# A streaming channel shuffle: the 8 KB tile is dropped, 4 and 28 KB share the first load buffer, and the last tile grows from 16 to 24 KB

## The chip, the cores and the metric

The kernel runs on one core of one Trainium2 chip. The metric is device time in microseconds (us) of one execution; the profile's span is about 1.8 us shorter than that time. Sizes such as "38 KB" are bytes per partition: 38 KB on 128 partitions is one transfer of 4864 KB. "Load" is HBM to SBUF, "store" is SBUF to HBM.

## The reference

```python
def reference(x, groups):                  # x: (16, 64, 64, 256) float32, groups = 8
    batch, h, w, c = x.shape
    x = x.reshape(batch, h, w, groups, c // groups)
    x = x.transpose(0, 1, 2, 4, 3)         # swap group and channel-in-group
    return x.reshape(batch, h, w, c)
```

Each pixel's 256 floats (1 KB) are permuted. 67.11 MB are read and 67.11 MB written, and nothing is computed.

## The kernel before

The input is cut into tiles. Each inner list of `_SLOTS` is one buffer's contents, and its numbers are KB per partition. A tile is loaded by SP's DMA queue, permuted by one vector-engine copy and stored by ACT's DMA queue. There are two load buffers and three store buffers, so a load waits for the copies of the slot two before it.

```python
_SLOTS = [[4, 8], [28]] + [[38]] * 12 + [[16]]
_IN_BUFS = 2
_OUT_BUFS = 3
# ... (pools, flat views, rows() cut)
for parts in _SLOTS:
    in_tile = in_pool.tile([P, biggest * c], F32, name="in_tile")
    out_tile = out_pool.tile([P, biggest * c], F32, name="out_tile")
    # ... (pieces: size, first row, columns)
    for q, start, cols in pieces:
        nc.sync.dma_start(out=in_tile[:, cols], in_=rows(x_flat, start, q))
    for q, start, cols in pieces:
        nc.vector.tensor_copy(out=out_tile[:, cols].rearrange("p (i j g) -> p i j g", j=CPG, g=G),
                              in_=in_tile[:, cols].rearrange("p (i g j) -> p i j g", g=G, j=CPG))
        nc.scalar.dma_start(out=rows(out_flat, start, q), in_=out_tile[:, cols])
```

Of the kernel before, what the change touches and what calls it, by code (L numbers as in the profile page):

```python
# [1 line left out]

# [4 lines left out]


F32 = mybir.dt.float32
P = 128  # L10

_SLOTS = [[4, 8], [28]] + [[38]] * 12 + [[16]]
_IN_BUFS = 2
_OUT_BUFS = 3


@with_exitstack
def kernel(
    ctx: ExitStack,
    tc: tile.TileContext,  # L20
    x: bass.AP,
    groups: bass.AP,
    out: bass.AP,
):
    nc = tc.nc
    b, h, w, c = x.shape
    G = int(groups)
    CPG = c // G
    assert G * CPG == c
    assert sum(map(sum, _SLOTS)) * P == b * h * w  # L30
    biggest = max(map(sum, _SLOTS))

    x_flat = x.rearrange("b h w c -> (b h w c)")
    out_flat = out.rearrange("b h w c -> (b h w c)")

    in_pool = ctx.enter_context(tc.tile_pool(name="in_pool", bufs=_IN_BUFS))
    out_pool = ctx.enter_context(tc.tile_pool(name="out_pool", bufs=_OUT_BUFS))

    def rows(flat, first, q):

        return flat[first * c : (first + P * q) * c].rearrange("(p f) -> p f", p=P)

    ctx.enter_context(tc.manual_schedule(engines=None))
    first = 0
# [3 lines that stand above are left out]
        at = 0  # L48
        pieces = []
        for q in parts:  # L50
            pieces.append((q, first, slice(at * c, (at + q) * c)))
            first += P * q
            at += q
# [3 lines that stand above are left out]
            nc.vector.tensor_copy(  # L57
                out=out_tile[:, cols].rearrange("p (i j g) -> p i j g", j=CPG, g=G),
                in_=in_tile[:, cols].rearrange("p (i g j) -> p i j g", g=G, j=CPG),
            )  # L60
            nc.scalar.dma_start(
                out=rows(out_flat, start, q), in_=out_tile[:, cols]
            )


# [1 line left out]
_INS = ['x', 'groups']  # L67
_OUTS = [((16, 64, 64, 256), 'float32')]

_NUMBERS = {'groups': 8}  # L70


# [26 lines left out]
```

## Time and profile before

| | before |
|---|---|
| median time | 316.1 us (3 runs at first: 316.08 to 316.41) |
| span of the profile | 314.4 us |
| HBM traffic over the span | 427 GB/s |
| vector engine busy | 38% |
| DMA engines, between first and last data packet | full |

The table says what to look at. Where the 16 DMA engines are the bound, the vector engine's idle time and the waits for loads cost nothing by themselves.

### The profile page before, as it was taken

How to read it: one execution, taken by the hardware profiler on the slowest of the kernel's cores; microseconds unless marked ns; L12 is line 12 of the kernel's file. 1: busy time of each engine (PE TensorE's matmuls, PEld its weight loads, DVE VectorE, ACT ScalarE, POOL GpSimd, SP SyncE). 2: the span in 40 equal slices, each digit the busy share in tenths (PEclk: the TensorE clock that was granted, in tenths of full speed). 3: DMA queues.
4: the chain of work that ended last, by engine and by line, in shares of the span. 5: the costliest groups of instructions: out<-in, count | busy, mean ns of one | idle time of the engine just before them, and what ended most of it. 6: DMA issues, size and time to landing. Idle time of an engine off the chain costs nothing.

```text
span 314.4 us, 132 instructions
## 1 busy us (share of the span) xinstructions
DVE 119.0 (38%) x16; POOL 0.2 (0%) x4
## 2 busy tenths in 40 slices
DVE  2081907309109109019028028037046055065400
POOL 0000000000000000000000000000000000000000
DMA  7999999999999999999999999999999999999997
GB/s 317 405 441 416 435 416 483 401 465 406 450 421 446 426 436 436 401 470 396 475 396 475 396 470 401 470 401 470 401 450 421 446 426 436 436 417 450 429 421 321
DMA packets 4608, 134.22 MB, mean 427 GB/s; under 512 B 512, under 2 KB 512, under 8 KB 768
## 3 DMA queue, kind: packets, MB, share of 16 engines
q1 hardware_dynamic: 2304, 67.11, 49.8%
q10 hardware_dynamic: 2304, 67.11, 49.4%
HBM read 67.11 MB, written 67.11 MB: 427 GB/s over the span
## 4 chain that ended last, share of the span: by engine, by line
DMA 76%; DVE 19%; issue 0%; SPq 0%; DVEq 0%
DMA in_tile<-in_x_dram 76%; DVE out_tile L57 19%; SPq L55 0%; DVEq L57 0%
## 5 line engine op out<-in xcount | busy, mean ns | idle before, releaser
L57 DVE COPY out_tile<-in_tile 128x9728 f32<-128x9728 f32 (+4 forms) x16 | 119.0, 7440 | 179.4 <-DMA in_tile<-in_x_dram 179.4
L80 POOL MEMSET const-uint8-127<- 128x1 uint8 x1 | 0.1, 103 | 0.0
L80 POOL MEMSET const-bfloat16-1.0<- 128x1 bf16 x1 | 0.1, 102 | 0.0
L80 POOL MEMSET const-float32-1.0<- 128x1 f32 x1 | 0.1, 100 | 0.0
L80 POOL MEMSET const-float32-0.0<- 128x1 f32 x1 | 0.1, 99 | 0.2 <-issue 0.2
## 6 DMA issues: line engine op xcount, KB each, us to landing
in_tile<-in_x_dram SPq DMA_DIRECT2D x12, 4864.0 KB, 37.0
out_dram<-out_tile ACTq DMA_DIRECT2D x12, 4864.0 KB, 42.6
in_tile<-in_x_dram SPq DMA_DIRECT2D x1, 3584.0 KB, 14.7
out_dram<-out_tile ACTq DMA_DIRECT2D x1, 3584.0 KB, 30.9
in_tile<-in_x_dram SPq DMA_DIRECT2D x1, 2048.0 KB, 30.4
out_dram<-out_tile ACTq DMA_DIRECT2D x1, 2048.0 KB, 15.2
in_tile<-in_x_dram SPq DMA_DIRECT2D x1, 1024.0 KB, 5.4
out_dram<-out_tile ACTq DMA_DIRECT2D x1, 1024.0 KB, 25.0
```

What stands on the lines that cost most here:

```text
L57: nc.vector.tensor_copy(out=out_tile[:, cols].rearrange("p (i j g) -> p i j g", j=CPG, g=G), in_=in_tile[:, cols].rearrange("p (i g j) -> ...
L80: nc = _bacc.Bacc("TRN2", target_bir_lowering=False, num_devices=1)
```

## The change

Its intent is one transfer pair less and more loads issued at once at the start, with the bytes of the 8 KB tile moved into the last tile.

```diff
-_SLOTS = [[4, 8], [28]] + [[38]] * 12 + [[16]]
+_SLOTS = [[4, 28]] + [[38]] * 12 + [[24]]
```

## The prediction

> **What bounds the kernel now.** I read the page first (parts 1 to 3), then the stretches of the execution, then the groups by form, then the end of the chain. Parts 2 and 3 say what kind of kernel this is:
>
> ```profile
> DVE  2081907309109109019028028037046055065400
> DMA  7999999999999999999999999999999999999997
> DMA packets 4608, 134.22 MB, mean 427 GB/s; under 512 B 512, under 2 KB 512, under 8 KB 768
> q1 hardware_dynamic: 2304, 67.11, 49.8%
> q10 hardware_dynamic: 2304, 67.11, 49.4%
> ```
>
> The vector engine works 38% of the span. The 16 DMA engines are busy in every slice but the first and the last, half for loads (q1) and half for stores (q10), 99.2% together. So the question is only whether any idle DMA time is left to win or to lose. The view by stretches cuts the span at the first and the last data packet (1.75 and 313.28 us in the trace's packet records; columns: stretch, length, vector busy, pool busy, clock, DMA share, GB/s):
>
> ```profile
> 0.00:1.75 1.75, 0.00 (x0) 0.20 (x4) 1.00 0.05 5
> 1.75:40.00 38.25, 18.50 (x4) 0.00 (x0) 1.00 1.02 425
> 40.00:280.00 240.00, 89.74 (x11) 0.00 (x0) 1.00 1.00 434
> 280.00:313.28 33.28, 10.80 (x2) 0.00 (x0) 1.00 0.97 417
> 313.28:314.40 1.12, 0.00 (x0) 0.00 (x0) 1.00 0.00 0
> ```
>
> 1.75 us pass before the first packet and 1.16 us after the last (314.44 - 313.28). The 311.53 us between are full: counting packets in flight on the 16 engines, idle time is 0.10 us (mean over engines) around 2 to 4 us, 0.03 us at 10 to 12 us, nothing from 12 to 312 us, and 0.4 us at the end, where the engines finish between 312.5 and 313.3 us. The lower 417 GB/s is that ragged end, 425 GB/s the slow first packets plus small packets.
>
> The page's chain gives 76% to loads and 19% to copies. It looks like a latency chain, and the waits seem to agree:
>
> ```profile
> DVE out_tile L57 <- DMA in_tile<-in_x_dram: 179.4, 16, 14.3
> ```
>
> That is an idle engine which is not the bottleneck: the copy waits because loads queue behind loads and share with stores. The tile period is 22.97 us (255.10 less 209.22 is two of them, 45.9), and 38 KB per partition in and out is 16 packets per engine of 1.439 us, 23.0 us. The period is the DMA engines' own time.
>
> **What the Trainium skill says.** "DMA: Bandwidth & Descriptors", section Specifications, gives a fabric ceiling of 435 GB/s and an HBM limit of about 358 GB/s per core. The trace runs at 434 GB/s in the middle, so the first figure is the one that binds here. The same page, section "Queues, rings and completion order", says each DMA engine takes turns between its queues packet by packet. The trace agrees: the 4 KB store is issued at 5.19 us, starts at 9.1 us and ends at 17.7 us, one of its packets to each load packet of 1.06 us. Section "Anatomy of one DMA" has a fixed cost near 2 us per transfer (fitted for the GpSimd path), mostly the receipt of the write. Here about 1 us passes from issue to first packet, and 0.3 us from the last packet of the first load to its landing, but with no idle engine between 12 and 312 us this is covered by the other transfers.
>
> **The change, part by part.** Bytes are unchanged (4+28+456+24 = 512 KB per partition, as 4+8+28+456+16). A transfer is 128 packets, one per partition, 8 per DMA engine. Median packet times in the records: 4 KB 159 ns, 8 KB 309, 16 KB 611, 28 KB 1062, 38 KB 1439. A line through the ends is 8.4 ns + 37.65 ns per KB, and it meets the three in the middle within 1 ns; 24 KB is therefore 912 ns (estimate from these).
>
> 1. Removed, the 8 KB tile: one load, one copy, one store. Per engine 2 x 8 x 0.309 = 4.94 us, and two completion packets of 9 ns.
> 2. Grown, the last tile from 16 to 24 KB: 2 x 8 x (0.912 - 0.611) = 4.82 us added.
> 3. Net on the full engines: 4.82 - 4.94 - 0.02 = **-0.15 us** (rounded from the unrounded terms). This is all packet overhead: 16 packets fewer at 8.4 ns, plus the completions.
> 4. Copies, from the groups by form:
>
> ```profile
> L57 DVE COPY out_tile<-in_tile 128x9728 f32<-128x9728 f32 x12 | 105.5, 8791 | 158.5 <-DMA in_tile<-in_x_dram 158.5
> L57 DVE COPY out_tile<-in_tile 128x7168 f32<-128x7168 f32 x1 | 6.6, 6569 | 7.7 <-DMA in_tile<-in_x_dram 7.7
> L57 DVE COPY out_tile<-in_tile 128x4096 f32<-128x4096 f32 x1 | 3.9, 3873 | 7.6 <-DMA in_tile<-in_x_dram 7.6
> L57 DVE COPY out_tile<-in_tile 128x2048 f32<-128x2048 f32 x1 | 2.0, 2019 | 1.5 <-DMA in_tile<-in_x_dram 1.5
> ```
>
> The 8 KB copy goes (2.02 us), the last grows from 3.87 to about 5.67 us (two thirds of the way from 16 to 28 KB). Both lie on the vector engine beside full DMA engines, so they count nothing unless they open a gap.
>
> 5. Moved, the start. Now the two buffers hold 12 and 28 KB, 40 KB of loads issued at once; the first 38 KB load waits for the 8 KB copy and is issued at 8.66 us. After, they hold 32 and 38 KB: 70 KB are issued at once, and the next load waits for the 28 KB copy. The 4 KB load ends at 3.7 us as now. The 28 KB load takes 8 x 1.062 = 8.5 us plus about three 4 KB store packets, to 12.7 us, landing at 13.0; its copy ends at 19.6 us, and then the third load and the 28 KB store are issued. The engines still have the first 38 KB load (8 x 1.439 = 11.5 us, plus the rest of the 4 KB store, 0.8 us), until 25 us. New work is ready about 1.4 us after its issue (0.33 for the issue, 1.0 to the first packet), at 21 us. **Spare: 4 us, so no gap.**
> 6. Moved, the end:
>
> ```profile
> 255.18 8.82 DVE out_tile L57
> 264.00 0.02 issue
> 264.01 30.41 DMA in_tile<-in_x_dram
> 294.42 0.03 issue
> 294.45 0.05 DVEq L57
> 294.50 0.04 issue
> 294.54 3.87 DVE out_tile L57
> ```
>
> This chain ends at 298.41 us, 16 us before the span does: what sets the end is the backlog of stores. The last store is issued at 298.45 us, and its first packet runs at 308.0, behind the previous 38 KB store. Ready at about 299.9, it has 8 us to spare. After: counted back from a last packet at 313.1 us, the 24 KB store needs 8 x 0.912 = 7.3 us (from 305.8), the 38 KB store before it 11.5 us (from 294.3). The 24 KB load must be done when only these two remain, so at 294.3 at the latest, landing at about 294.6; copy to 300.4, first packet ready at 301.8. **Spare: 4 us.** Half of the slack goes, and none of it shows.
>
> Sum: 1.75 + 311.53 - 0.15 + 1.16 = 314.3 us of span, and 316.1 - 0.15 = **316.0 us** of time.
>
> **The rivals.** (a) *The removed fixed costs count:* two transfers at the skill's 2 us would give about 312 us. For it, the small tiles stand at the start, where few transfers are queued. Against it, idle DMA time there is 0.13 us in all, so nothing of the kind is exposed. (b) *A new wait starves the start:* the third load now waits on the 28 KB copy instead of the 8 KB one. If the 4 us of spare were wrong and the engines waited from 12.7 us for work issued at 19.6, it would cost up to 8 us, 324 us. Against it, the first 38 KB load needs no such wait: its buffer is fresh. (c) *The larger last tile is exposed at the end:* with no store backlog it would add 1.8 us of copy and 8 x 0.301 = 2.4 us of store, some 320 us. Against it, the backlog of 18.8 us above. (d) *The start's disturbances change:* the first packets of the 4 KB load took up to 679 ns instead of 159, and the 28 KB load's packets add up to 0.26 us over their median. Fewer, larger transfers could move this by some tenths either way; so could the raggedness of the end (0.8 us).
>
> **Range and chances.** The core of it is -0.15 us with (d) of about 0.4 us on either side, and the runs before spread 0.33 us (316.08 to 316.41). That gives 315.4 to 316.5 us. Two per cent is 6.3 us: more than all idle time inside and outside the packets (about 3.4 us), so faster by that is next to impossible, 0.005. Slower needs (b) fully, or (b) and (c) together, 0.01. Within 2%: 0.985.
>
> **What would show it.** DMA digits of 9 from the second slice to the last but one; 434 GB/s from 40 to 280 us; first packet still near 1.75 us; 28 KB landing near 13 us, third load issued near 19.6 us; last load landing near 294.5 us and a last copy near 5.7 us, ending some 14 us before the span. An idle DMA stretch of over 0.5 us near 20 to 26 us, or between the last two stores near 306 us, would prove me wrong, and a DMA packet of 38 KB that takes other than 1.44 us would too.

## The result, and the profile after

The change takes **317.59 us** (median of 6 runs, 316.71 to 318.46), the kernel before in the same rounds 316.1 us (6 runs, 316.08 to 316.41). The ratio is 1.0044, with a 95% interval of 1.0025 to 1.0062; ratios here are the mean time of one kernel's fast runs over that of the other's of the same rounds, so not quite the ratio of the medians quoted. It is clearly not faster, and it lies above the predicted range of 315.4 to 316.5 us. The runs also spread over 1.75 us, those of the kernel before over 0.33.

Parts 2 and 3 of the page of the change:

```profile
DMA  8998999999999999999999999999999999999996
GB/s 346 388 464 357 432 453 429 443 429 438 429 438 429 448 419 448 419 448 419 448 414 453 414 453 414 453 409 458 409 458 409 458 404 468 399 460 396 444 429 264
DMA packets 4320, 134.22 MB, mean 425 GB/s; under 512 B 480, under 2 KB 480, under 8 KB 736
q1 hardware_dynamic: 2160, 67.11, 49.7%
q10 hardware_dynamic: 2160, 67.11, 49.2%
```

The engines are as full as before, 98.9% of a longer span. One slice stands out: the fourth (23.7 to 31.6 us), with 357 GB/s and a DMA digit of 8. The view by stretches of the change, cut at its own first and last data packets (columns: stretch, length, vector busy, pool busy, clock, DMA share, GB/s):

```profile
1.74:40.00 38.26, 16.46 (x3) 0.00 (x0) 1.00 1.02 419
40.00:280.00 240.00, 88.39 (x10) 0.00 (x0) 1.00 1.00 434
280.00:314.73 34.73, 14.63 (x2) 0.00 (x0) 1.00 0.94 407
314.73:316.00 1.27, 0.00 (x0) 0.00 (x0) 1.00 0.00 0
```

The middle is the same 434 GB/s. The loss is at both ends: 419 instead of 425 GB/s up to 40 us, and 407 instead of 417 at the end, where the last packet ends at 314.73 us instead of 313.28.

Start, in finer stretches, of the kernel before:

```profile
20.00:28.00 8.00, 2.93 (x1) 0.00 (x0) 1.00 1.11 471
28.00:44.00 16.00, 8.82 (x1) 0.00 (x0) 1.00 0.98 412
```

and of the change:

```profile
20.00:28.00 8.00, 0.23 (x1) 0.00 (x0) 1.00 0.93 348
28.00:44.00 16.00, 8.76 (x1) 0.00 (x0) 1.00 1.03 444
```

The DMA share counts time in packets, the last column bytes. Their quotient is what busy engines move: 348 / 0.93 = 374 GB/s in the change between 20 and 28 us, and 444 / 1.03 = 431 right after. The engines are busy and move less. Against the 434 GB/s of the middle, that is 0.93 x 8 us x (1 - 374/434) = 1.0 us of full-speed time lost. In the kernel before the two quotients are 424 and 420 GB/s, some 0.2 and 0.5 us by the same working. (A packet counts in the stretch in which it starts, so a share can lie above 1 or a little below without an idle engine.)

The packet records show what this is. Nearly every packet of a size takes the same time (38 KB: 1.439 us); those that don't are mostly at the start. In the change, 16 load packets of 38 KB, one for each engine by their count (the records don't name the engine), are stretched by 0.8 to 1.07 us, to as much as 2.51 us, between 23.4 and 27.8 us; three more were stretched by 0.4 us just before. The 16 are the last packets of the first 38 KB load, and by the times, on 13 of the engines the packet that follows is the first of the 28 KB store; on the other three the store's first packet ran ahead of the load's last. Before, there are 16 such packets too, stretched by 0.25 to 0.41 us near 33 us, in the middle of a 38 KB load, again just ahead of the first 28 KB store packet. From here on, "stretch" is the sum over packets that start between 12 and 60 us of their time less the median of their size, divided by 16: **0.58 us before, 1.02 us in the change**.

The copies, in the view of groups by form of the change, are what they were, with the new 24 KB one in its place:

```profile
L57 DVE COPY out_tile<-in_tile 128x9728 f32<-128x9728 f32 x12 | 106.1, 8841 | 163.1 <-DMA in_tile<-in_x_dram 163.1
L57 DVE COPY out_tile<-in_tile 128x6144 f32<-128x6144 f32 x1 | 5.7, 5691 | 9.9 <-DMA in_tile<-in_x_dram 9.9
```

The 38 KB copies take 8.84 us instead of 8.79, with the vector engine still mostly waiting for loads, so the copies are not where the time went. End of the chain of waits of the change:

```profile
266.50 32.69 DMA in_tile<-in_x_dram
299.19 0.03 issue
299.21 0.05 DVEq L57
299.26 0.04 issue
299.31 5.69 DVE out_tile L57
```

The last load lands at 299.19 us. A transfer is complete when its 16 engines' shares have all landed, and the records have each share. For this load the median share lands at 296.29 us; three engines are 2.5 to 2.9 us later. From the first 38 KB load on, landing at 27.4 us, every load has three shares that come 1.6 us or more after the median. By itself that is a matter of order and not of lost time: in a later look at the same kernel (the first of the two more looks below) every 38 KB load has shares over 1 us late too, and its last store ends within 0.20 us of its median share. What is lost shows in the last store. Of the last store the median share lands at 313.65 us (before 313.27) and the last one at 315.08 (before 313.62). So 0.38 us is common to all engines, and 1.08 us (1.43 less 0.35) is that three engines end late. 316.22 us, the profiled run before, plus these is 317.68; the profiled run of the change took 317.79.

### The profile page after: what moved, and what is told of

Same layout as the page of the kernel before. It is cut to its first block, busy times and chain, and to the rows that moved or that the text cites. A ratio compares the mean times of both kernels' runs of the same rounds, so it can differ in the third digit from the quotient of the medians.

```text
span 316.0 us, 126 instructions
## 1 busy us (share of the span) xinstructions
DVE 119.5 (38%) x15; POOL 0.2 (0%) x4
## 3 DMA queue, kind: packets, MB, share of 16 engines
q1 hardware_dynamic: 2160, 67.11, 49.7%
q10 hardware_dynamic: 2160, 67.11, 49.2%
## 4 chain that ended last, share of the span: by engine, by line
DMA 77%; DVE 19%; SPq 0%; issue 0%; DVEq 0%
DMA in_tile<-in_x_dram 77%; DVE out_tile L57 19%; SPq L55 0%; DVEq L57 0%
## 5 line engine op out<-in xcount | busy, mean ns | idle before, releaser
L57 DVE COPY out_tile<-in_tile 128x9728 f32<-128x9728 f32 (+3 forms) x15 | 119.5, 7965 | 185.5 <-DMA in_tile<-in_x_dram 185.5
## 6 DMA issues: line engine op xcount, KB each, us to landing
out_dram<-out_tile ACTq DMA_DIRECT2D x12, 4864.0 KB, 31.6
in_tile<-in_x_dram SPq DMA_DIRECT2D x1, 3072.0 KB, 32.7
```

## The experiments

The theory to be tested (A) is that the loss is made at the start: the 28 KB store enters an engine that for a while has had loads only, at a bad moment, which stretches load packets and sets engines apart. The rivals are the larger last tile (B) and the shared buffer (C); later, the missing 8 KB load instead of the missing 8 KB store (D). All runs gave correct results. The first four went together, the kernel before taking 316.19 us (11 runs, 316.01 to 317.32) beside them.

**Changed start alone.**

```diff
-_SLOTS = [[4, 28]] + [[38]] * 12 + [[24]]
+_SLOTS = [[4, 28]] + [[38]] * 12 + [[8]] + [[16]]
```

> Changed start alone: 4 and 28 KB share the first load buffer, and the tail ends in an 8 and a 16 KB tile, so the last store is 16 KB as before. Theory A (the loss is made at the start, where the store queue runs dry between the 4 KB and the 28 KB store, 19.5 to 24.2 us, the load packets then stretch by about 1 us on every engine and three engines fall out of step): as slow as the change, 317.0 to 318.5 us, stretched load packets near 22 to 28 us, engines ending 1 us or more apart. Theory B (the larger last tile makes the ragged end): 316.1 us, engines ending within 0.5 us.

Measured 320.56 us (319.47 to 321.58), ratio 1.0132. The stretch is 0.91 us, as A says, with packets up to 2.50 us; but no engine falls out of step here (last share of the last store 0.07 us after the median). The total misses both expectations because the cut tail costs 3 us of its own:

```profile
306.00:312.50 6.50, 3.90 (x1) 0.00 (x0) 1.00 0.55 231
```

The 16 KB load is issued at 286.98 us, shares its engines packet by packet with 38 KB stores and lands at 306.88; its copy ends at 310.90, when the other stores have landed (309.31). The engines are 45% idle. This is what the prediction's rival (c) describes, made by a badly chosen tail; as a verdict on B the run is spoiled, but its start counts.

**Changed tail alone** (with the 28 KB tile cut to 20 KB, so that the bytes add up).

```diff
-_SLOTS = [[4, 8], [28]] + [[38]] * 12 + [[16]]
+_SLOTS = [[4, 8], [20]] + [[38]] * 12 + [[24]]
```

> Changed tail alone: 24 KB last tile, start kept as 4 and 8 KB in one buffer, then 20 KB in the other. Theory A (start): about 316.1 us, stretch of a load packet by 0.4 us or less, engines ending within 0.5 us. Theory B (tail): 317 us or more with engines ending over 1 us apart.

Measured 316.52 us (316.14 to 316.98), ratio 1.0006 (0.9992 to 1.0019). Stretch 0.59 us. A last tile of 24 KB costs nothing measurable: B falls for this size. Some engines end up to 0.7 us late, a bit more than A expected.

**The 8 KB tile kept, all three in the first buffer.**

```diff
-_SLOTS = [[4, 28]] + [[38]] * 12 + [[24]]
+_SLOTS = [[4, 8, 24]] + [[38]] * 12 + [[20]]
```

> Three tiles share the first buffer, 4, 8 and 24 KB, then 38 KB tiles, 20 KB last: the 8 KB tile stays, the sharing of the buffer stays. Theory A (the store queue runs dry because the 8 KB store is missing): about 316.2 us, since the 8 KB store fills the gap. Theory C (the sharing itself, 70 KB of loads ahead and a later third load, costs): 317 us or more.

Measured 316.33 us (five runs 316.27 to 316.46, one 318.32), ratio 1.0012 (0.9992 to 1.0032). Stretch 0.61 us. Sharing the buffer is harmless: C falls. The one slow run is the profiled one: its last store's median share lands at 313.33 us, the last at 315.72. One engine was 2.4 us late, 15 were not.

**The sizes of the change, not shared.**

```diff
-_SLOTS = [[4, 28]] + [[38]] * 12 + [[24]]
+_SLOTS = [[4], [28]] + [[38]] * 12 + [[24]]
```

> The sizes of the change, but 4 and 28 KB in a buffer each, so that the first 38 KB load waits for the 4 KB copy (issued near 5.2 us instead of 1.6 us). Theory A: the store queue still runs dry between the 4 and the 28 KB store, so 317 to 318.5 us with the stretch at 22 to 28 us. Theory C (sharing): 316.1 us.

Measured 316.88 us (316.57 to 318.56), ratio 1.0033 (1.0011 to 1.0055). Stretch 0.89 us. Its stretch of time:

```profile
20.00:28.00 8.00, 0.24 (x1) 0.00 (x0) 1.00 0.93 352
```

That is 379 GB/s for busy engines, as in the change. This refutes C a second time: the sizes bring the loss, not the sharing.

The next four had the kernel before at 316.1 us (11 runs, 316.02 to 316.33) beside them. They ask what about the entry costs: that the store queue had run dry (A1), or that it meets the end of one load and the start of the next (A2).

**The boundary between loads moved.**

```diff
-_SLOTS = [[4, 28]] + [[38]] * 12 + [[24]]
+_SLOTS = [[4, 28]] + [[30]] + [[38]] * 11 + [[32]]
```

> The start of the change with a 30 KB tile in place of the first 38 KB one, 32 KB last. The first big load now ends near 22.5 us, before the 28 KB store enters, so the store enters in the middle of the next load. Theory A1 (a 28 KB store entering a dry store queue costs about 1 us whatever the load queue does): full-speed time lost between 20 and 40 us near 1.0 us per engine, as in the change. Theory A2 (about 0.4 us of it is the entering store, as before the change, and the other 0.6 us comes from meeting the boundary between two loads): near 0.4 us.

> The 30 KB second tile once more, timed in rounds: whether 328.5 us stands (it was one run). Locked phase: 326 to 329 us with store packets near 1.57 us. If it was a chance of that run: 316 to 318 us.

Measured 328.54 us in one look, and when timed later 329.0 us (327.52 to 329.26; before 316.13), ratio 1.0398. Nobody expected this. Up to 30 us it goes as A2 says: the store enters one packet after the boundary (24.5 us; the 30 KB load's packets end at 22.9), and the load packets there are stretched by 0.53 and 0.58 us per engine in the two profiles, nearer to A2's 0.4 than to A1's 1.0. But then the whole middle is slow (second profile):

```profile
60.00:280.00 220.00, 79.44 (x9) 0.00 (x0) 1.00 1.00 412
```

The engines are full and move 412 GB/s instead of 434. In the records the median 38 KB store packet takes 1.57 us instead of 1.44, while load packets keep 1.44. The two queues have locked: every load and a store of the same size end within 0.3 us of each other, tile after tile, whereas before the change they end 5.7 us apart.

**The lock broken.** The same sizes, with the 28 KB tile copied and stored in two pieces (the edit of "store split" below).

> The 30 KB second tile as in the earlier run of 328.5 us, with the 28 KB tile stored as 8 and 20 KB. If the 12 us there come from the phase in which the load and store queues lock (loads and stores ending together, store packets of 1.57 us instead of 1.44), the other start of the store queue breaks the lock: 316.2 to 317 us and store packets of 1.44 us. If they come from the sizes 30 and 32 KB: again near 328 us.

Measured 316.94 us (316.41 to 317.06), store packets of 1.44 us again. So the sizes 30 and 32 don't cost the 12 us by themselves. That the phase between the queues does is the reading left, tested by this one variant. Why this phase slows stores was not found.

**24 KB first.**

```diff
-_SLOTS = [[4, 28]] + [[38]] * 12 + [[24]]
+_SLOTS = [[4, 24]] + [[38]] * 12 + [[28]]
```

> 4 and 24 KB share the first buffer, 28 KB last: the 24 KB store is issued near 17.5 us and enters the store queue near 20 us, in the middle of the first 38 KB load, two packets or so before that load ends, and nearly without a dry store queue. A1: loss between 16 and 40 us near 0.8 to 1.0 us if the store queue was dry for over 2 us. A2: near 0.4 us.

> 4 and 24 KB in the first buffer and 28 KB last, timed in rounds: the 8 KB tile is gone and the last tile is larger still, but the store enters in the middle of a load. A2: 316.0 to 316.4 us, as the kernel before. If the removal of the 8 KB tile or the larger last tile cost anything by itself: 316.6 us or more.

Measured 316.21 us in one look; timed later 316.86 us (316.18, 316.21, 316.27, 317.45, 317.55, 318.65), ratio 1.0029. Stretch 0.55 and 0.46 us. With no 8 KB tile and an even larger last one, the entry costs what it cost before the change; it falls a packet or two before the load's end, as expected. But the median of 316.86 us is on the side that was written down for a cost of the missing 8 KB tile or of the larger last tile (316.6 us or more): half of the runs sit at the level of the kernel before, the other half 1.3 us or more above it. The profile is of the 317.45 us run, and here the tail does show:

```profile
303.00:307.00 4.00, 1.42 (x1) 0.00 (x0) 1.00 0.66 278
```

One engine was 1.6 us late, so the 28 KB load landed at 297.65 us; the copy of 6.66 us put the last store at 304.45, and 14 to 15 of the engines had nothing from about 304.5 to 305.3 us. So here a late engine delayed all the others, since the last tile left too little spare.

**Store split.** Loads as in the change; the 28 KB tile is copied and stored as 8 and 20 KB.

```diff
+_CUTS = {28: [8, 20]}
...
-            nc.vector.tensor_copy(... all columns of the piece ...)
-            nc.scalar.dma_start(... all columns of the piece ...)
+            for r in _CUTS.get(q, [q]):
+                nc.vector.tensor_copy(... the next r KB ...)
+                nc.scalar.dma_start(... the next r KB ...)
```

> The change with its loads as they are, but the 28 KB tile copied and stored in two pieces of 8 and 20 KB, so the store queue gets 8 KB packets near 17 us and hardly runs dry. Theory A: the loss at 22 to 28 us falls from 1.0 to 0.5 us or less, and the time to 316.0 to 316.4 us, like the kernel before. Theory D (it is the missing 8 KB load, not the missing store, that does it): as slow as the change, 317 to 318.5 us.

Measured 316.42 us (five runs 316.32 to 316.72, one 318.72), ratio 1.0026 (1.0004 to 1.0047). Stretch 0.58 us. The 8 KB load stays away and the stretch goes back to its size before the change: for the stretch, D falls; it is the store. The median is just above what A expected, and a slow run remains, so D is not refuted for the slow runs (see the end of the next part).

**The change again**, for its spread.

> The change itself once more, for its spread on the same chip as the split store. All theories: 316.7 to 318.5 us; the loss near 24 us is again 0.9 to 1.1 us per engine in its trace, and the time between runs differs by how far single engines fall behind at the end.

Measured 316.63 us (316.47 to 318.03), ratio 1.0024, a little under what was expected. Stretch 0.96 us. Last store: median share 313.69 us, last 314.36; the profiled run took 317.07.

**Store delayed.** The cleanest test of A1 against A2: the loads and sizes of the change, only the time of entry moved.

```diff
             nc.vector.tensor_copy(...)
+            if q == 28:
+                for _ in range(2):
+                    nc.vector.tensor_copy(out=out_tile[:, cols], in_=out_tile[:, cols])
             nc.scalar.dma_start(...)
```

> The change, with two more copies of the 28 KB output tile onto itself before its store, so that the store enters some 7 us later, in the middle of the second 38 KB load; loads are not held up. A1 (the loss grows with the time that the store queue is dry): 1.0 us or more lost between 20 and 44 us. A2 (the loss comes from entering where one load ends and the next begins): 0.4 to 0.6 us. Time after A2: some 316.2 us, unless the queues lock into a bad phase as they did with the 30 KB tile.

Measured 316.56 us (316.39 to 317.05), ratio 1.0012 (0.9998 to 1.0027), some 0.4 us more than A2 expected. The store is issued at 28.05 us instead of 20.26 and enters at 32.7, in the middle of the second 38 KB load:

```profile
20.00:28.00 8.00, 7.93 (x4) 0.00 (x0) 1.00 1.00 433
28.00:44.00 16.00, 10.81 (x3) 0.00 (x0) 1.00 1.00 417
```

The 374 GB/s of the change are 433 now, and the later entry costs 16 x (1 - 417/434) = 0.6 us. Stretch 0.57 us, although the store queue was dry for 13 us (19.7 to 32.7) instead of 4.7 to 6.7. The last store's median share lands at 313.29 us, as before the change (313.27); one engine ends 1.05 us after it, and that is most of what the profiled run of 317.05 us has over the kernel before. A1 falls, A2 stands. This is the run that tells them apart: in the others whose store enters within a load, the store queue was also dry for less time (1 to 5 us by engine).

**Two more looks at the change, and two last variants.** What lifts its runs from 316.5 to 318.5 us was still open.

> The change, one more look. The loss where the 28 KB store enters is again near 1.0 us per engine. What exceeds 316.5 us is then lateness of single engines: the last landing of the last store minus the median one should grow with the time, and, if a run above 318 us falls here, either that, or idle DMA engines ahead of the last store, near 306 us.

> The change, a second look, same reading as the first: 0.9 to 1.1 us lost at the entry, time above 316.5 us explained by engines that end late or by a gap near 306 us.

Measured 316.67 and 316.65 us; stretch 1.02 and 0.90 us; last store's shares 313.75 and 313.95, 313.68 and 313.94 us (median, last). With the engines together at the end, the change costs 0.45 and 0.43 us over the profiled run before (316.22 us), which is what the median share shows (later by 0.48 and 0.41 us). The two looks brought no run above 318 us, so for those they decide nothing directly.

The variant with both the 28 KB store and the last tile cut (`_CUTS = {28: [8, 20], 24: [12, 12]}`):

> The change with the 28 KB store in 8 and 20 KB and the 24 KB tile copied and stored in two halves, so the last store is ready some 2.8 us earlier. If the runs above 318 us come from a last store that is issued too late when an engine lags: none above 317.3 us, median 316.3 us. If they come from the lagging engines themselves: a run or two of six above 317.3 us as with the 28 KB store split alone.

Measured 317.2 us (316.31 to 318.74, 5 runs), so an earlier last store does not take the slow runs away. Its profile is of the 318.74 us run: last store's median share 313.34 us, last one 316.15, two engines 2.2 and 2.8 us late, the other 14 within 0.4 us, and no hole ahead of the last store. Here the excess is late engines and nothing else.

The kernel before with its 28 KB store in 8 and 20 KB:

> The kernel before with its 28 KB store in 8 and 20 KB, as a candidate: if smaller first store packets reduce the loss at the entry (0.57 us in the kernel before), 315.9 to 316.1 us; if the loss only moves, 316.1 to 316.4 us.

Measured 316.08 us (316.02 to 316.68) beside 316.16 for the kernel before, ratio 0.9999 (0.9986 to 1.0011). Stretch 0.53 us: it moved to the next entry near 50 us. Nothing tried beats the kernel before by a measurable amount.

Together, by where the large store enters ("within a load" is ahead of the load's last packets; the last column is the landing of the last store's median share):

| kernel | store enters | stretch, us | fastest run, us | median share, us |
|---|---|---|---|---|
| before | within a load | 0.58 | 316.01 | 313.27 |
| before, store split | within a load | 0.53 | 316.02 | 313.24 |
| changed tail alone | within a load | 0.59 | 316.14 | 313.38 |
| 8 KB kept, shared | within a load | 0.61 | 316.27 | 313.33 |
| 24 KB first (two profiles) | within a load | 0.55, 0.46 | 316.18 | 313.25, 314.27 (the hole above) |
| store split | within a load | 0.58 | 316.32 | 313.44 |
| both split | within a load | 0.60 | 316.31 | 313.34 |
| store delayed | within a load | 0.57 | 316.39 | 313.29 |
| change (four profiles) | at the end of a load | 1.02, 0.96, 1.02, 0.90 | 316.47 | 313.65, 313.69, 313.75, 313.68 |
| not shared | at the end of a load | 0.89 | 316.57 | 313.65 |

Left out are the three kernels with a loss of their own later on: the changed start (stretch 0.91 us, at the end of a load), the moved boundary (0.84 and 0.99, of which 0.53 and 0.58 at the entry) and the moved boundary with the store split (0.70).

The common part of the loss adds up. With the packets before 12 us counted as well, time over the median of the size is 1.15 us per engine before and 1.67 to 1.74 in the four profiles of the change, so 0.52 to 0.59 more; less the 0.15 us of work saved, that is 0.37 to 0.44. The median share of the last store lands 0.38 to 0.48 us later.

## Why the prediction was wrong

**Right.** The bound: full DMA engines, 434 GB/s in the middle before and after. No idle stretch at the start: packets in flight show less than 0.1 us of idle time between 10 and 312 us, as before. Landing of the 28 KB load near 13 us (13.6), issue of the third load near 19.6 (20.26), last copy 5.67 us (5.69), first packet at 1.74 us. The time is within 2% of the kernel before, as forecast. A saving of 0.15 us was never tested by itself, but the sum above comes out closer with it. Rivals (a) and (b) did not happen.

**The step that failed** is part 3, "Net on the full engines ... -0.15 us", with the assumption under it that a full engine is a fast one: that each packet takes the median of its size. The falsifier was named in the last sentence, "a DMA packet of 38 KB that takes other than 1.44 us", and it is what came: 2.51 us. The working checked that the engines had work near 20 to 26 us and did not ask what the moved entry of the 28 KB store would do to the packets beside it, although the trace before already had the same event, 0.25 to 0.41 us per engine near 33 us. Rival (d) names only the disturbances of the 4 and 28 KB loads, before 16 us. Part 5 also had new work ready 1.4 us after its issue, at 21 us. The store, issued at 20.26 us, sent its first packet at 24.2, 3.9 us later; the 4 KB store that the prediction quotes took as long (5.19 to 9.1 us), and 3.9 us after the predicted issue (19.6 us) is 23.5, among the last packets of the first 38 KB load, which it had ending at 25 us.

**A term under-sized.** Rival (d) put the start's disturbances and the ragged end at about 0.4 us either way. Measured: the stretch rises by 0.32 to 0.44 us (0.90 to 1.02, from 0.58), always upward; entering at the end of a load cost more than within one in every profile. The median of the first six runs rose by 1.49 us, so this is the smaller part of it. In the profile that followed the prediction the ragged end added 1.08 us more; over the four profiles of the change the last share trails the median by 1.43, 0.67, 0.20 and 0.26 us. The two fastest runs of the change, 316.47 and 316.50 us, are at the top of the predicted range; all 14 runs of it are at 316.47 us or more.

**A step wrong that did not cost here.** Part 6 gave the last store 4 us of spare by reasoning that the last load must land at 294.6 us "at the latest", all stores but two being done. The queues need not keep that order. In the change the stores are ahead of the loads: the store before the last two lands at 293.9 us (median share), the last load at 296.3, and at 299.2 on the late engines, where 294.5 was forecast; the last copy ended 11 us before the span's end instead of 14. The last store was issued at 305.03 us, and its first packets ran at 305.9, with the store before it just ending: about no spare at all. The 28 KB variant shows the cost when it falls short, some 1 us.

**What stays open.** Why a load packet stretches when a store joins it, and why by about 1 us at a load's end and half of it inside a load, no run shows. Nor why some engines fall behind: in the slow profiles one or two packets per tile stretch by 0.1 to 0.7 us while the others keep their time, and runs of one kernel differ in it. That late engines account for the profiled runs of 317.79, 318.32 and 318.74 us is shown by their landings; for the unprofiled slow runs of the change it is only likely. One unprofiled run of the kernel before was at 317.32 us, so it is not immune. The slow runs do not follow the stretch but go with the missing 8 KB load: over 317 us were 19 of the 46 runs without that load (the kernels with a loss of their own, changed start and moved boundary, left out), with a small stretch or a large one, and 2 of the 55 with it (1 of 38 of the kernel before). No experiment was made to test this, so for the slow runs rival D stands.

## What to carry to other kernels

On a kernel whose DMA engines are full, divide bytes by busy share stretch by stretch: a busy engine that moves less is invisible in the busy digits, and it is where a re-tiling can lose what its packet count wins. When tiles at the start are merged or dropped, work out at which packet of the load queue the first large store will enter, and whether loads and stores will end together from then on; here 0.4 us went with the one and 12 us with the other, with the same bytes. And judge such a change by its spread as well as its median: in the slow runs that were profiled, one to three late engines of 16 set the end.

## What the Trainium skill lacked or had wrong

- "DMA: Bandwidth & Descriptors", section "Queues, rings and completion order", has engines taking turns packet by packet, with which the traces agree (loads 49.7% and stores 49.2% of the engines' time), but nothing on what a packet takes when the other queue joins: load packets of 1.44 us were stretched by 0.25 to 0.41 us before the change and by up to 1.14 us after it, when the first large store entered.
- No page has that stores can be slowed while two queues run in step: with loads and stores ending together, 38 KB store packets took 1.57 us instead of 1.44, 412 GB/s instead of 434, 12 us of 316.
- "DMA: Bandwidth & Descriptors", section "Latency and other measured facts", notes that two of the 16 engines are usually slower in traces and gives a guess tied to descriptors written by GpSimd, which issues no transfer here. It has nothing on engines falling behind in some runs and not in others: the last share of the last store came 0.1 to 2.8 us after the median one, with 16 shares of equal size in every transfer, and the time followed.
